# Moving operands of a one-core transformer block placed 32 to 224 bytes further on in a 256-byte line

## The chip, the cores and the metric

The kernel runs on one core of one Trainium2 chip. The metric is the device time in microseconds of one execution, as the median of several. TensorE (PE in the profile) multiplies a weight tile that it has loaded with a moving operand that it reads from SBUF column by column; the result goes to PSUM. VectorE (DVE) and ScalarE (ACT) do the element-wise work, and the queue of SyncE (SP) issues the loads from HBM.

## The reference

One layer over 512 tokens of width 1024: an input projection, a state-space mixer and a dilated attention side by side, both gated and projected back, a gated feed-forward part of width 2816 with a causal convolution of three taps, and a last gated addition.

```python
u = rms_norm(h, mix_norm_g)
z = u @ w_in                       # 1024 -> 512 + 3 * 768 + 2 * 1024
y_a = s5_mixer(z[:, :512], ...) @ w_branch_a     # inside: y * sigmoid(y @ glu_w + glu_b)
y_b = dilated_attention(q, k, v) @ w_branch_b
h = h + (g_a * y_a + g_b * y_b) @ w_out
u2 = rms_norm(h, ffn_norm_g)
gate = causal_depthwise_conv(u2 @ ffn_w_gate, ffn_conv_w, ffn_conv_b)
h = h + (gelu(gate) * (u2 @ ffn_w_up)) @ ffn_w_down
u3 = rms_norm(h, ple_norm_g)
h = h + sigmoid(u3 @ ple_w_gate) * (p @ ple_w_proj)
return rms_norm(h, final_norm_g)
```

## The kernel before

Activations lie in SBUF with 128 features on the partitions and all 512 tokens along the row, as float32. Every large product is made three times: each operand is split into a high part in TensorE's fp32r format and the rest as a low part, and `mm3` (lines 148 to 151) adds high times high (L149), high times low (L150) and low times high (L151). So each of the 128x128 weight tiles serves two matmuls with its high part and one with its low part, and each matmul has a weight load of its own.

The weights come in 132 chunks of 128x1024 floats through `wprep` (lines 115 to 131): a load into `wr`, ACT makes `wh` from it (L128), DVE makes `wl` (L129), three buffers of each in a ring. `gemm` takes eight weight tiles of 512 bytes a row out of a chunk, one after the other. The stages, in order, with the names that the rows show as result<-moving,weights:

- `pa`: five projections by tokens. Here the roles are the other way round: the weight chunk `wh`/`wl` moves, 512 columns of it, and slices of the activation `u1h`/`u1l` are loaded as weights.
- `v` and `gps`: the rest of the input projection, `u1h`/`u1l` moving. The small matmuls of the state-space mixer and of attention are woven in between by a list of background work that the program order fixes.
- `lps`: the mixer's gate, `yh`/`yl` moving; `bpb`: attention's projection, `bx` moving; `bpa`: the mixer's projection, `zh`/`zl` moving; `ops`: the output projection, `mh`/`ml` moving.
- twice (`part`): `pg` and `pu`, eleven pairs of feed-forward products with `u2h`/`u2l` moving, and `dps`, with `ah`/`al` moving.
- `pps`, with `px_` moving, and `eps`, with `u3h`/`u3l` moving; the last two rows of tiles of `eps` run in two halves of 256 columns each.
- `n_ps`, twice: a sum over partitions, `n_hi` and then `n_lo` moving, with the constant `ones_r` as weights (L241, L242).

The large activations lie in tagged slots of one pool (`slot`, line 76), used again by later stages. In the built program each slot, each `wr`, `wh`, `wl` and each 2 KB temporary, `n_hi` and `n_lo` among them, begins 64 bytes past a multiple of 256 in its partition's row; all steps from one tile to the next within them are multiples of 512 bytes. So weights and moving operand of each `mm3` begin at the same place in a line of 256 bytes. The constants `ones_r` and `cst` begin 160 and 224 bytes past a multiple of 256. `cst` is the weights of `shp` (L645), three small float32 products of the mixer's preparation, whose moving operand `pz` begins at 64.

Of the kernel before, what the change touches and what calls it, by code (L numbers as in the profile page):

```python
# [10 lines left out]
F32R = mybir.dt.float32r  # L11
# [9 lines left out]
SEQ = 512  # L21
# [22 lines left out]
STATS_AT = (7, 0)  # L44
NLAST = 2
LAST = ((0, 1), (2, 3))
LN2_HI = 0.693359375
LN2_LO = -2.12194440e-4

# [15 lines left out]
def tile_hybrid_block(ctx: ExitStack, tc: tile.TileContext, xT, xtok, pT, W, vecs, consts, ssm, out):  # L65
# [10 lines left out]
    def slot(i, shape, name, dt=F32):  # L76
        return sb.tile([P] + shape, dt, tag=f"s{i}", name=name)

    def small(shape, name, dt=F32):
        return sm_.tile([P] + shape, dt, tag=name, name=name)  # L80

    def mm_tile(name):
        return pm.tile([P, 512], F32, tag="mm", name=name)
# [4 lines left out]
    def t_tile(name):  # L88
        return ring.tile([P, 512], F32, tag="t", name=name, bufs=4)


    vec = small([V_N], "vec")
    nc.scalar.dma_start(vec, vecs)
    ones = small([128], "ones")
    DVE.memset(ones, 1.0)
    warm = small([1], "warm")
    ACT.activation(warm, ones[:, 0:1], AF.Sqrt)
    x = slot("x", [KD, SEQ], "x")
# [3 lines left out]
    def v1(col):  # L102
        return vec[:, col:col + 1]
# [47 lines left out]
        PE.matmul(ps, st[1], mv[0], start=False, stop=last)  # L151

    def u_tiles(name):
        uh = [slot(f"uh{j}", [4, SEQ], f"{name}h{j}", F32R) for j in range(2)]
        ul = [slot(f"ul{j}", [4, SEQ], f"{name}l{j}", F32R) for j in range(2)]
        return ([uh[k // 4][:, k % 4, :] for k in range(KD)], [ul[k // 4][:, k % 4, :] for k in range(KD)])

    def u_split(u, k, src, gcol, c=slice(0, SEQ)):
        ACT.activation(u[0][k][:, c], src[:, c], AF.Copy, scale=v1(gcol + k))  # L159
        DVE.scalar_tensor_tensor(u[1][k][:, c], src[:, c], v1(gcol + k), u[0][k][:, c].bitcast(F32), op0=ALU.mult, op1=ALU.subtract)  # L160
# [11 lines left out]
    def first():  # L172
        for c in (slice(0, 128), slice(128, SEQ)):
            nc.sync.dma_start(x[:, 0, c], xT[:, 0, c])
            u_split(u, 0, x[:, 0, :], V_MIX, c)

    u = u_tiles("u1")
    ready.append(wprep(2, first))
    load_x(1)
# [19 lines left out]
    def sq_acc(acc, k, src):  # L199
        if k == 0:  # L200
            ACT.activation(acc, src, AF.Square)
        else:
            t = t_tile("sq")
            ACT.activation(t, src, AF.Square)
            DVE.tensor_tensor(acc, acc, t, op=ALU.add)
# [29 lines left out]
    def rstd_full(acc, name):  # L235
        hi = ring.tile([P, SEQ], F32R, tag="t", name=name + "_hi", bufs=4)
        lo = ring.tile([P, SEQ], F32R, tag="t", name=name + "_lo", bufs=4)
        ACT.activation(hi, acc, AF.Copy)
        DVE.tensor_tensor(lo, acc, hi.bitcast(F32), op=ALU.subtract)
        ps = ax_tile(name + "_ps")  # L240
        PE.matmul(ps, ones_r, hi, start=True, stop=False)  # L241
        PE.matmul(ps, ones_r, lo, start=False, stop=True)  # L242
        m = t_tile(name + "_m")
        DVE.tensor_scalar(m, ps, 1.0 / D, EPS, op0=ALU.mult, op1=ALU.add)
        t = t_tile(name + "_t")
        ACT.activation(t, m, AF.Sqrt)
        y = sb.tile([P, SEQ], F32, tag="acc", name=name + "_y")
        DVE.reciprocal(y, t)
        DVE.tensor_tensor(t, y, y, op=ALU.mult)
        DVE.tensor_tensor(t, t, m, op=ALU.mult)  # L250
        DVE.tensor_scalar(t, t, -0.5, 1.5, op0=ALU.mult, op1=ALU.add)
        DVE.tensor_tensor(y, y, t, op=ALU.mult)
        return y
# [43 lines left out]
    S = slot("S", [NQ, 2, R, H], "S")  # L297
# [107 lines left out]
    def gemm(ps, kt, mv):  # L405
        for k in range(kt):
            mm3(ps, wT.next(), (mv[0][k], mv[1][k]), k == 0, k == kt - 1)
# [4 lines left out]
    def tt(o, a, b, op):  # L412
        DVE.tensor_tensor(o, a, b, op=op)  # L413
# [7 lines left out]
    def stt(o, a, s, b, o0, o1):  # L421
        DVE.scalar_tensor_tensor(o, a, s, b, op0=o0, op1=o1)

    def g_ssm():
# [12 lines left out]
        def rint(o, a, s):  # L437
            ts(o, a, s, ALU.mult, MAGIC, ALU.add)
            ts(o, o, -MAGIC, ALU.add)

        def exp_(o, a):
            xx, n, n1, r, q = e1, e2, e3, e4, e5
            ts(xx, a, -170.0, ALU.max, 170.0, ALU.min)
            rint(n, xx, LOG2E)
            stt(r, n, -LN2_HI, xx, ALU.mult, ALU.add)
            stt(r, n, -LN2_LO, r, ALU.mult, ALU.add)
# [439 lines left out]
    def split(hi, lo, src):  # L886
        ACT.activation(hi, src, AF.Copy)
        tt(lo, src, hi.bitcast(F32), ALU.subtract)

    yh = slot("S", [4, SEQ], "yh", F32R)  # L890
    yl = slot("f0", [4, SEQ], "yl", F32R)
    for k in range(4):
        split(yh[:, k, :], yl[:, k, :], yT[:, k, :])
    zh = slot("uh0", [4, SEQ], "zh", F32R)
    zl = slot("ul0", [4, SEQ], "zl", F32R)

    def parts(t, n):
        return [t[:, k, :] for k in range(n)]
# [1 line left out]
    for m in range(4):  # L900
        ps = mm_tile("lps")
        gemm(ps, 4, (parts(yh, 4), parts(yl, 4)))
        t = t_tile("lg")
# [8 lines left out]
    h = slot("x", [KD, SEQ], "h")  # L912
# [21 lines left out]


    u2 = u_tiles("u2")
    acc2 = sb.tile([P, SEQ], F32, tag="acc", name="acc2")
    for m in range(KD):
# [9 lines left out]
        DVE.memset(e[:, 0:2, 0:1], 0.0)  # L948
    u3 = None
    for part in range(2):  # L950
        ah = [slot(n, [4, SEQ], f"ah{part}{j}", F32R) for j, n in enumerate(("g0", "g1", "f0"))]
        al = [slot(n, [4, SEQ], f"al{part}{j}", F32R) for j, n in enumerate(("T", "f1", "S"))]
        a_h = [ah[k // 4][:, k % 4, :] for k in range(HALF)]
        a_l = [al[k // 4][:, k % 4, :] for k in range(HALF)]
        for mi in range(HALF):
            m = part * HALF + mi
            pg = mm_tile("pg")
            gemm(pg, KD, u2)
            if m == 0:
                rb2 = rstd_full(acc2, "n2")  # L960
            pu = mm_tile("pu")
            gemm(pu, KD, u2)
            e = exts[m % 2]
            tt(e[:, 2:6, :], pg.rearrange("p (r i) -> p r i", r=R), rb2.rearrange("p (r i) -> p r i", r=R), ALU.mult)
            ACT.activation(e[:, 0:2, 1:128], e[:, 4:6, 0:127], AF.Copy)
            t = t_tile("cv")
            t3 = t.rearrange("p (r i) -> p r i", r=R)
            ACT.activation(t3, e[:, 2:6, :], AF.Identity, bias=v1(V_CB + m), scale=v1(V_CW + 44 + m))
            stt(t3, e[:, 1:5, :], v1(V_CW + 22 + m), t3, ALU.mult, ALU.add)
            stt(t3, e[:, 0:4, :], v1(V_CW + m), t3, ALU.mult, ALU.add)  # L970
            ACT.activation(t, t, AF.Gelu_apprx_tanh)
            t2_ = t_tile("up")
            tt(t2_, pu, rb2, ALU.mult)
            tt(t, t, t2_, ALU.mult)
            split(a_h[mi], a_l[mi], t)
        if part == 1:
            u3 = u_tiles("u3")
            acc3 = sb.tile([P, SEQ], F32, tag="acc", name="acc3")
        for m in range(KD):
            ps = mm_tile("dps")  # L980
            gemm(ps, HALF, (a_h, a_l))
            tt(h[:, m, :], ps, h[:, m, :], ALU.add)
            if part == 1:
                u_split(u3, m, h[:, m, :], V_PLE)
                sq_acc(acc3, m, h[:, m, :])
# [67 lines left out]
    waiting = []  # L1053
    for gi, rs in enumerate(LAST):
        c = slice(rs[0] * 128, rs[-1] * 128 + 128)
        end = gi == len(LAST) - 1
        for m in tail:
# [19 lines left out]
    n = 0  # L1077
    for rs, y in zip(LAST, y4):
        for j in range(2):
# [153 lines left out]
```

## Time and profile before

| | |
|---|---|
| median of 3 runs | 808.01 us (807.91 to 808.68) |
| the profiled execution's own time | 807.97 us |
| its span, first to last instruction | 806.2 us |
| PE busy | 795.8 us, 4294 matmuls |
| PEld, weight loads | 659.8 us, 4294 loads |
| DVE busy | 489.8 us |
| ACT busy | 346.3 us |
| HBM read | 76.18 MB |

The profile is one execution. A matmul's record runs from its first column to a modelled end, after the next matmul has begun; so the records overlap, and the time from one start to the next is shorter than a record. A weight load (PEld) runs beside the matmul before its own.

### The profile page before, as it was taken

To read this page: it belongs to the slowest core of one execution; us is meant where nothing else is said; L and a number is where in the kernel's file an instruction comes from. 1 tells how busy PE (TensorE), PEld (TensorE's weight loads), DVE (VectorE), ACT (ScalarE), POOL (GpSimd) and SP (SyncE) were. 2 spreads that over 40 slices of the span, in tenths; PEclk is the share of its full clock that TensorE was granted. 3 is DMA by queue.
4 is the path that set the end of the run, shared out by engine and by line. 5 is a ranking of instruction groups with operands and counts; after the bars stand their busy time and mean duration, and the time that the engine had idled before them with its cause. 6 is when DMAs were issued, how large, how long until landed. Compare 5 with 4: busy or idle time off the path is not lost.

```text
span 806.2 us, 10860 instructions
## 1 busy us (share of the span) xinstructions
PE 795.8 (99%) x4294; PEld 659.8 (82%) x4294; DVE 489.8 (61%) x944; ACT 346.3 (43%) x551; POOL 10.9 (1%) x10
## 2 busy tenths in 40 slices
PE   9999999999999999999999999999999999999996
PEld 7888888788787788888888888888888888888886
DVE  6974799932544548756866556323655655445576
ACT  6763634434443533434544433221443443335464
POOL 2001000000000000000000000000000000000000
PEclk9999999999999999999999999999999999999999
DMA  7721121231111132533232232233223223222202
GB/s 272 273 91 62 46 93 63 80 105 53 53 54 54 53 105 81 206 105 114 96 105 91 93 104 96 88 104 105 80 103 105 95 89 104 99 87 102 102 4 104
DMA packets 23810, 78.97 MB, mean 98 GB/s; under 512 B 2640, under 2 KB 3024, under 8 KB 23760
## 3 DMA queue, kind: packets, MB, share of 16 engines
q1 hardware_dynamic: 23616, 78.22, 28.4%
q8 instruction: 33, 0.54, 0.3%
q14 instruction: 17, 0.14, 0.1%
q10 hardware_dynamic: 144, 0.07, 0.0%
HBM read 76.18 MB, written 2.10 MB: 97 GB/s over the span
## 4 chain that ended last, share of the span: by engine, by line
PE 86%; DVE 9%; ACT 2%; issue 1%; DMA 1%; SPq 0%; DVEq 0%; ACTq 0%
PE pu L151 5%; PE dps L151 5%; PE pg L151 5%; PE dps L150 5%; PE pu L149 5%; PE pu L150 5%; PE pg L149 5%; PE pg L150 5%; PE dps L149 5%; PE gps L149 4%; PE gps L151 4%; PE gps L150 4%; PE pa L151 2%; PE pa L150 2%; DVE E L413 2%; PE pa L149 2%
## 5 line engine op out<-in xcount | busy, mean ns | idle before, releaser
L128 ACT ACTIVATE wh<-wr 128x1024 fp32r<-128x1024 f32 (+1 forms) x132 | 138.1, 1047 | 302.0 <-issue 64.4
L129 DVE TENSOR_TENSOR wl<-wr,wh 128x1024 fp32r<-128x1024 f32 (+1 forms) x132 | 159.2, 1206 | 69.4 <-ACT wh L128 69.1
L150 PE MATMUL pu<-u2l,wh 128*128 128x512 f32 x176 | 68.5, 389 | 0.0
L149 PE MATMUL pu<-u2h,wh 128*128 128x512 f32 x176 | 68.5, 389 | 0.0
L149 PE MATMUL pg<-u2h,wh 128*128 128x512 f32 x176 | 68.5, 389 | 0.0
L150 PE MATMUL pg<-u2l,wh 128*128 128x512 f32 x176 | 68.5, 389 | 0.0
L151 PE MATMUL dps<-ah,wl 128*128 128x512 f32 x176 | 68.5, 389 | 0.0
L150 PE MATMUL dps<-al,wh 128*128 128x512 f32 x176 | 68.5, 389 | 0.0
L151 PE MATMUL pg<-u2h,wl 128*128 128x512 f32 x176 | 68.5, 389 | 0.0
L151 PE MATMUL pu<-u2h,wl 128*128 128x512 f32 x176 | 68.5, 389 | 0.0
L149 PE MATMUL dps<-ah,wh 128*128 128x512 f32 x176 | 68.5, 389 | 0.0
L149 PE MATMUL pa<-wh,u1h 128*128 128x512 f32 x160 | 63.2, 397 | 0.8 <-ACT u1h L159 0.7
L150 PE MATMUL pa<-wl,u1h 128*128 128x512 f32 x160 | 62.7, 392 | 0.0
L151 PE MATMUL pa<-wh,u1l 128*128 128x512 f32 x160 | 62.4, 392 | 0.1
L149 PE MATMUL gps<-u1h,wh 128*128 128x512 f32 x128 | 51.3, 401 | 0.0
L151 PE MATMUL gps<-u1h,wl 128*128 128x512 f32 x128 | 50.5, 395 | 0.0
L150 PE MATMUL gps<-u1l,wh 128*128 128x512 f32 x128 | 50.2, 392 | 0.0
L413 DVE TENSOR_TENSOR ext<-pg,n_y 128x512 f32<-128x512 f32 x22 | 15.2, 692 | 44.1 <-PE pg L151 44.1
L413 DVE TENSOR_TENSOR gt<-gps,n_bc 128x512 f32<-128x512 f32 x16 | 11.1, 692 | 50.7 <-PE gps L151 50.7
L150 PEld LDWEIGHTS dps<-al,wh 128*128 128x128 f32 x176 | 33.0, 188 | 6.9
L150 PEld LDWEIGHTS pu<-u2l,wh 128*128 128x128 f32 x176 | 33.0, 188 | 6.9
L150 PEld LDWEIGHTS pg<-u2l,wh 128*128 128x128 f32 x176 | 33.0, 188 | 6.9
(305 smaller groups left out, 1535.8 us busy)
## 6 DMA issues: line engine op xcount, KB each, us to landing
wr<-in_W_dram SPq DMA_DIRECT2D x128, 512.0 KB, 3.2
xt<-in_xtok_dram SPq DMA_DIRECT2D x4, 512.0 KB, 7.9
h<-in_xT_dram SPq DMA_DIRECT2D x8, 256.0 KB, 4.7
out_dram<-fo SPq DMA_DIRECT2D x8, 256.0 KB, 2.3
x<-in_xT_dram SPq DMA_DIRECT2D x7, 256.0 KB, 5.7
wr<-in_W_dram SPq DMA_DIRECT2D x4, 256.0 KB, 5.7
cst<-in_consts_dram SPq DMA_DIRECT2D x1, 568.0 KB, 10.4
sp<-in_ssm_dram SPq DMA_DIRECT2D x1, 544.0 KB, 7.5
```

What stands on the lines that cost most here:

```text
L128: ACT.activation(hi[:, c], raw[:, c], AF.Copy)
L129: DVE.tensor_tensor(lo[:, c], raw[:, c], hi[:, c].bitcast(F32), op=ALU.subtract)
L149: PE.matmul(ps, st[0], mv[0], start=first, stop=False)
L150: PE.matmul(ps, st[0], mv[1], start=False, stop=False)
L151: PE.matmul(ps, st[1], mv[0], start=False, stop=last)
L413: DVE.tensor_tensor(o, a, b, op=op)
```

## The change

A helper `moved` makes the tile 256 bytes longer than its content and lets the content begin `off` floats into it. The tiles `u1`, `u2`, `u3` (all three through `u_tiles`), `y`, `z` and `a` are made with it, at 32, 56, 8 and 16 floats: 128, 224, 32 and 64 bytes. The weights, `mh`/`ml`, `bx`, `px_`, `n_hi` and `n_lo` stay as they were. In the built program the instructions of each engine are the same and in the same order as before. Ten slots become 256 bytes longer, so that everything behind them lies some multiple of 256 bytes further on, and its place in a line of 256 bytes is unchanged. In `pa` the weights lie 128 bytes further on and the moving chunk does not; in the other stages it is the moving operand.

```diff
+U_OFF, Y_OFF, Z_OFF, A_OFF = 32, 56, 8, 16
...
+    def moved(tag, kt, name, off):
+
+        t = slot(tag, [kt * SEQ + 64], name, F32R)
+        return t[:, off:off + kt * SEQ].rearrange("p (k n) -> p k n", k=kt)
...
     def u_tiles(name):
-        uh = [slot(f"uh{j}", [4, SEQ], f"{name}h{j}", F32R) for j in range(2)]
-        ul = [slot(f"ul{j}", [4, SEQ], f"{name}l{j}", F32R) for j in range(2)]
+        uh = [moved(f"uh{j}", 4, f"{name}h{j}", U_OFF) for j in range(2)]
+        ul = [moved(f"ul{j}", 4, f"{name}l{j}", U_OFF) for j in range(2)]
...
-    yh = slot("S", [4, SEQ], "yh", F32R)
-    yl = slot("f0", [4, SEQ], "yl", F32R)
+    yh = moved("S", 4, "yh", Y_OFF)
+    yl = moved("f0", 4, "yl", Y_OFF)
...
-    zh = slot("uh0", [4, SEQ], "zh", F32R)
-    zl = slot("ul0", [4, SEQ], "zl", F32R)
+    zh = moved("uh0", 4, "zh", Z_OFF)
+    zl = moved("ul0", 4, "zl", Z_OFF)
...
-        ah = [slot(n, [4, SEQ], f"ah{part}{j}", F32R) for j, n in enumerate(("g0", "g1", "f0"))]
-        al = [slot(n, [4, SEQ], f"al{part}{j}", F32R) for j, n in enumerate(("T", "f1", "S"))]
+        ah = [moved(n, 4, f"ah{part}{j}", A_OFF) for j, n in enumerate(("g0", "g1", "f0"))]
+        al = [moved(n, 4, f"al{part}{j}", A_OFF) for j, n in enumerate(("T", "f1", "S"))]
```

## Rows read from the trace of the kernel before

**Rows 1.** The page's head: span, and busy time by engine.

```profile
span 806.2 us, 10860 instructions
PE 795.8 (99%) x4294; PEld 659.8 (82%) x4294; DVE 489.8 (61%) x944; ACT 346.3 (43%) x551; POOL 10.9 (1%) x10
```

**Rows 2.** All waits of PE: who for whom, total us, times, longest.

```profile
PE qkT L392 <- DVE qk L386: 1.6, 4, 0.8
PE warm L165 <- DVE apw L526: 1.0, 1, 1.0
PE pa L149 <- ACT u1h L159: 0.7, 2, 0.4
```

**Rows 3.** Busy time by stretch: us, PE busy (matmuls), granted clock, DMA share, GB/s.

```profile
0.00:20.00 20.00, 18.13 (x74) 1.00 0.77 271
20.00:40.00 20.00, 20.00 (x90) 1.00 0.74 272
520.00:540.00 20.00, 20.00 (x90) 1.00 0.26 84
```

**Rows 4.** The tile dps, 500 to 596 us: records min/median/max, first to last start.

```profile
L149 PE MATMUL dps<-ah,wh x87: 389/389/390, 499.7 to 558.2; 128*128 128x512 f32 x87
...
L151 PEld LDWEIGHTS dps<-ah,wl x87: 187/188/188, 499.9 to 558.4; 128*128 128x128 f32 x87
```

**Rows 5.** The tile shp: float32 matmuls of 256 columns, the same columns.

```profile
L645 PE MATMUL shp<-pz,cst x6: 378/379/380, 69.5 to 70.6; 128*128 128x256 f32 x6
```

**Rows 6.** The tile eps from 782 to 795 us: fp32r in halves.

```profile
L149 PE MATMUL eps<-u3h,wh x33: 277/283/389, 781.9 to 794.6; 128*128 128x256 f32 x32, 128*128 128x512 f32 x1
```

**Rows 7.** The tile n_ps, both times.

```profile
L241 PE MATMUL n_ps<-n_hi,ones_r x2: 392/392/393, 384.3 to 754.9; 128*128 128x512 f32 x2
L242 PE MATMUL n_ps<-n_lo,ones_r x2: 390/390/390, 384.5 to 755.1; 128*128 128x512 f32 x2
```

**Rows 8.** The tile pu, 384.7 to 386.7 us, just behind n_ps.

```profile
L149 PE MATMUL pu<-u2h,wh x3: 393/396/397, 384.7 to 386.1; 128*128 128x512 f32 x3
...
L150 PE MATMUL pu<-u2l,wh x3: 393/397/398, 385.0 to 386.4; 128*128 128x512 f32 x3
...
L151 PE MATMUL pu<-u2h,wl x3: 387/389/389, 385.2 to 386.6; 128*128 128x512 f32 x3
```

**Rows 9.** PE's groups of L149 by shape: count, busy us, mean ns, idle before.

```profile
L149 PE MATMUL pu<-u2h,wh 128*128 128x512 f32 x176 | 68.5, 389 | 0.0
L149 PE MATMUL pg<-u2h,wh 128*128 128x512 f32 x176 | 68.5, 389 | 0.0
L149 PE MATMUL dps<-ah,wh 128*128 128x512 f32 x176 | 68.5, 389 | 0.0
L149 PE MATMUL pa<-wh,u1h 128*128 128x512 f32 x160 | 63.2, 397 | 0.8 <-ACT u1h L159 0.7
L149 PE MATMUL gps<-u1h,wh 128*128 128x512 f32 x128 | 51.3, 401 | 0.0
L149 PE MATMUL ops<-mh,wh 128*128 128x512 f32 x64 | 24.9, 389 | 0.0
L149 PE MATMUL eps<-u3h,wh 128*128 128x512 f32 x48 | 18.7, 390 | 0.0
L149 PE MATMUL bpa<-zh,wh 128*128 128x512 f32 x32 | 12.5, 389 | 0.0
L149 PE MATMUL eps<-u3h,wh 128*128 128x256 f32 x32 | 9.1, 285 | 0.0
L149 PE MATMUL v<-u1h,wh 128*128 128x512 f32 x16 | 6.4, 400 | 0.0
L149 PE MATMUL bpb<-bx,wh 128*128 128x512 f32 x16 | 6.2, 390 | 0.0
L149 PE MATMUL pps<-px__5861,wh 128*128 128x512 f32 x16 | 6.2, 390 | 0.0
L149 PE MATMUL lps<-yh,wh 128*128 128x512 f32 x16 | 6.2, 389 | 0.0
```

## The prediction

> **What bounds the kernel now.** I read the page's head first: PE is busy in 795.8 of 806.2 us, DVE in 61% and ACT in 43% of the span [rows 1]. A busy PE need not be a PE at its peak, so the second view is its waits: 3.3 us in all, in seven places [rows 2]. No other engine and no transfer sets the pace after the first 20 us; a stretch in the middle has PE busy throughout, at a granted clock of 1.00 (the 2.4 GHz level) and with the DMA engines at 0.26 [rows 3]. So the time is the number of matmuls times the distance from one start to the next, and the question is what that distance consists of.
>
> For it I take one tile in a steady stretch. In `dps` the first and the last of 87 L149 matmuls start at 499.7 and 558.2 us, and between two of them stand one L150 and one L151: 58.5 us / (86 x 3) = 226.7 ns from start to start [rows 4]. The record of each is 389 ns, so a record outlasts the next start by about 162 ns, and differences between records can be read as differences between steps. The halves of `eps`, with 256 columns, have a median record of 283 [rows 6]: 256 columns more cost 106 ns, 0.414 ns each, one cycle at 2.4 GHz. 512 columns are then 213.3 ns, and about 13 ns of every step come once per matmul, whatever its columns. The weight load under it takes 188 ns [rows 4] and ends before the step does; it isn't the bound itself. But it comes once per matmul too, and it reads SBUF while the moving operand is read.
>
> Is the 13 ns a constant of the engine? Three rows say that it isn't quite. `shp`, float32 at half the pace of columns, has a record of 379, 10 ns less, and its moving operand, at 64, starts 96 bytes behind its weights, at 224, counted round a 256-byte line [rows 5]. `n_ps` takes its weights from `ones_r`, so that `n_hi`, at 64, starts 160 bytes behind them: its record is 392 both times, and the next is 390 [rows 7]. The `pu` matmuls right after it, back at distance 0, have records from 387 to 398 before they settle at 389 [rows 8], without any wait that the view of waits names there. So the step depends on how weight load and moving stream meet: 389 is where a long run at distance 0 settles, and records of this shape between 387 and 398 exist.
>
> **The change, part by part.** It adds and removes no instruction. ACT and DVE write the moved tiles at another start, with the same shapes; I cost that at nothing, under the 57% and 39% of the span in which these engines are idle [rows 1]. Without that cover a changed write would have to add more than the slack, and no row shows one that depends on its start. Ten slots 256 bytes longer cost nothing in time.
>
> What is left is the step of the matmuls whose distance changes. Each group of L149 has two like it, of L150 and L151, so three times the counts [rows 9]: with 512 columns `pu` 528, `pg` 528, `pa` 480, `gps` 384, `eps` 144, `v` 48, and `eps` in halves 96, together 2208 at distance 128; `dps` 528 at 64; `lps` 48 at 224 and `bpa` 96 at 32. That is 2880. Not moved are `ops` 192, `bpb` 48, `pps` 48.
>
> Price of one, from both sides. The best is the 379 of `shp`: 10 ns less [rows 5]. The worst is the 398 seen behind `n_ps`: 9 ns more [rows 8]. Nearer than either lie the shortest records of the same kind: 387 against 389 for 512 columns [rows 8], 277 against 283 for 256 [rows 6], 2 and 6 ns less. I take their mean, 4 ns less, for distance 128, which is as far from the weights as a 256-byte line allows; half of it, 2, for 64; a quarter, 1, for 32 and 224, which are 32 bytes away on either side. This proportion is my choice; no row fixes it.
>
> - distance 128: 2208 x 4 ns = 8.8 us
> - distance 64: 528 x 2 ns = 1.1 us
> - distances 32 and 224: 144 x 1 ns = 0.1 us
>
> Together 10.0 us less. Of the `pa` matmuls, those of the first 40 us run while the DMA engines are 0.74 to 0.77 busy [rows 3]; if the loads set the pace there, some 150 of them give nothing, 0.6 us, inside the rounding of the price. Elsewhere ACT and DVE have to bring the chunks 1.2% sooner, which their idle time allows. The profiled execution took 807.97 us, 1.8 us outside its span, and agrees with the median, 808.01; so 808.0 - 10.0 = **798.0 us**.
>
> **The rivals.**
>
> No change, 808. The weight load may have its own way into SBUF, and the 13 ns be the price of putting a new set of weights in place in this format. For it: all long runs settle at exactly 389, whatever slot, chunk buffer or stage [rows 9], though other address bits vary between them. The group means above 389, in `pa`, `gps` and `v`, come from stages with small matmuls woven in. Against it: rows 5, 7 and 8. The Trainium skill speaks for this rival: its page "TensorE: Matmul & The Clock Gate", in "Step-by-step: what each phase is for", gives PE two independent read ports and says that loading the next weights takes no SBUF bandwidth from the running matmul. By that rule the distance would be worth nothing and the time 808.0; the trace agrees only so far that the load is hidden, 188 ns in a step of 226.7.
>
> The whole excess goes, 779. Any distance other than 0 takes the two streams apart and the record falls to the 379 of `shp`: 2880 x 10 ns = 28.8 us, 779.2 us. For it: `shp` is the one full-width row at another distance with a long run of columns. Against it: it is float32, which reads its columns at half the pace, and `n_hi` at 160 is longer, not shorter.
>
> Slower, 817. The new distances settle above 389. The mechanism is the one of rows 7: the first fp32r matmul that this trace shows at a distance other than 0 has a record 3 ns longer, both times. At 3 ns each, 2880 x 3 = 8.6 us, 816.6 us; if the streams settled at the longest record, 9 ns, 833.9 us. It decides from the point at which the record of `pu` and `pg` lies above 389; these and the others at distance 128 are three quarters of all moved. Against it: two single matmuls at the start of a disturbance, which then swings to 387 as well, don't tell where a long run would settle.
>
> **How the numbers follow.** Partial gain 0.40, the whole excess 0.17, no change 0.19, slower 0.24. Anything within 0.2% (1.6 us) can't be told from no change. Faster is 0.40 + 0.17 = 0.57, same 0.19, slower 0.24. The partial gain's own range is 785 to 805. The range from 779 to 817 goes from the whole excess to 3 ns more per matmul; outside remain a gain past the record of `shp` and the part of the slower case beyond 392, together not over 0.2.
>
> **What the profile after would show.** The controls are in the kernel: `ops`, `bpb` and `pps` keep their distance and must stay at 389 or 390, and the record of `n_hi`, unmoved too, at about 392. Right would be: records of `pu`, `pg` and the 512-column `eps` near 385, `dps` near 387, `bpa` and `lps` near 388, with weight loads still near 188 and PE's waits still a few us. If they all stand at 389 and the time at 808, the excess isn't a meeting of the two streams, or doesn't hang on their distance in 256 bytes. If `pu` falls to 379, the price was too small by 6 ns. If it rises to 392 or more, the sign was wrong: distance 0 was already one of the better places. If the moved groups differ in another order than 128, 64, 32, the proportion is wrong. And if records fall but the span doesn't, a feeder has become the bound: DVE's `wl` (L129) or the loads of `wr` would then stand among PE's waits.

## The result and the profile after: slower by 1.5%

| | before | after |
|---|---|---|
| median, 4 runs each | 808.35 us (807.91 to 809.49) | 820.53 us (819.59 to 821.68) |
| span of the profiled execution | 806.2 us | 818.3 us |

The ratio is 1.0149, with a 95% interval of 1.0132 to 1.0167. The forecast was 798.0 us, in a range from 779 to 817.

The head of the page and all waits of PE after the change, to be read beside [rows 1, 2]:

```profile
span 818.3 us, 10860 instructions
PE 808.5 (99%) x4294; PEld 660.8 (81%) x4294; DVE 490.7 (60%) x944; ACT 346.7 (42%) x551; POOL 10.9 (1%) x10
```

```profile
PE warm L172 <- DVE apw L533: 1.0, 1, 1.0
PE qkT L399 <- DVE qk L393: 0.7, 2, 0.5
PE pa L156 <- ACT u1h L166: 0.6, 1, 0.6
PE pa L157 <- DVE u1l L167: 0.3, 1, 0.3
```

PE is 12.7 us busier, with the same 4294 matmuls and 2.6 us of waits instead of 3.3. ACT, DVE and the weight loads are as busy as before to within 1 us. So nothing new is waited for, and PE alone works clearly longer. The granted clock in a middle stretch is 1.00 as before (columns: stretch, its length, PE busy with its count, clock, DMA share, GB/s):

```profile
520.00:540.00 20.00, 20.00 (x90) 1.00 0.32 106
```

The groups of PE by shape, as [rows 9] (lines 149 to 151 are now 156 to 158):

```profile
L158 PE MATMUL pg<-u2h,wl 128*128 128x512 f32 x176 | 69.5, 395 | 0.0
L156 PE MATMUL pu<-u2h,wh 128*128 128x512 f32 x176 | 69.5, 395 | 0.0
...
L157 PE MATMUL dps<-al,wh 128*128 128x512 f32 x176 | 69.3, 394 | 0.0
L156 PE MATMUL dps<-ah,wh 128*128 128x512 f32 x176 | 69.0, 392 | 0.0
L158 PE MATMUL dps<-ah,wl 128*128 128x512 f32 x176 | 68.3, 388 | 0.0
L156 PE MATMUL pa<-wh,u1h 128*128 128x512 f32 x160 | 63.7, 400 | 0.7 <-ACT u1h L166 0.6
...
L156 PE MATMUL gps<-u1h,wh 128*128 128x512 f32 x128 | 51.7, 404 | 0.0
...
L156 PE MATMUL ops<-mh,wh 128*128 128x512 f32 x64 | 24.9, 389 | 0.0
...
L156 PE MATMUL eps<-u3h,wh 128*128 128x512 f32 x48 | 18.9, 395 | 0.0
L156 PE MATMUL bpa<-zh,wh 128*128 128x512 f32 x32 | 12.7, 396 | 0.0
L156 PE MATMUL eps<-u3h,wh 128*128 128x256 f32 x32 | 9.1, 284 | 0.0
...
L156 PE MATMUL bpb<-bx,wh 128*128 128x512 f32 x16 | 6.4, 398 | 0.0
L157 PE MATMUL pps<-px__5861,wh 128*128 128x512 f32 x16 | 6.3, 396 | 0.0
L156 PE MATMUL lps<-yh,wh 128*128 128x512 f32 x16 | 6.3, 396 | 0.0
```

Every moved group of 512 columns is longer, and `ops`, which was not moved, is at 389 as before. That the step (the time from one start to the next) grew, and not only the modelled record, is read from the first and last starts of one tile (columns: min/median/max, first to last start). The first row is `pg` in the second part after the change, the second the same of the kernel before; eleven groups of 24 matmuls with ten `pu` groups between make 501 steps from the first to the last L156:

```profile
L156 PE MATMUL pg<-u2h,wh x88: 390/393/404, 566.8 to 683.2; 128*128 128x512 f32 x88
```

```profile
L149 PE MATMUL pg<-u2h,wh x88: 389/389/390, 558.8 to 672.4; 128*128 128x512 f32 x88
```

116.4 us / 501 = 232.3 ns against 113.6 / 501 = 226.7. For `dps`, in the first part, and the two matmuls of `n_ps`:

```profile
L156 PE MATMUL dps<-ah,wh x88: 392/392/397, 506.3 to 566.1; 128*128 128x512 f32 x88
L157 PEld LDWEIGHTS dps<-al,wh x88: 188/188/188, 506.3 to 566.1; 128*128 128x128 f32 x88
...
L158 PE MATMUL dps<-ah,wl x88: 388/388/398, 506.8 to 566.5; 128*128 128x512 f32 x88
```

```profile
L248 PE MATMUL n_ps<-n_hi,ones_r x2: 389/389/389, 388.7 to 766.6; 128*128 128x512 f32 x2
...
L249 PE MATMUL n_ps<-n_lo,ones_r x2: 397/397/397, 389.0 to 766.8; 128*128 128x512 f32 x2
```

`dps`: 59.8 us / 261 steps = 229.1 ns, and its three lines differ steadily, 392, 394 and 388: the stage has settled into a repeating pattern, where before all three were 389 [rows 4]. The weight loads take 188 ns as before.

The sum by records: `pg` and `pu` 1056 x 5.7 ns = 6.0 us; `pa` 480 x 4.0 = 1.9; `gps` 384 x 3.7 = 1.4; `eps` in full width 144 x 5.0 = 0.7; `dps` 528 x 2.3 = 1.2; `lps` and `bpa` 144 x 6.3 = 0.9; `v` 48 x 4.3 = 0.2; `bpb`, unmoved, 48 x 3.7 = 0.2; and the halves of `eps` 96 x 1.7 = 0.2 less (means over the three lines of each). Together 12.3 us; the span grew by 12.1.

### The profile page after: what moved, and what is told of

Read it like the earlier page. It is cut to its first block, busy times and chain, and to the rows that moved or that the text cites. A ratio compares the mean times of both kernels' runs of the same rounds, so it can differ in the third digit from the quotient of the medians.

```text
span 818.3 us, 10860 instructions
## 1 busy us (share of the span) xinstructions
PE 808.5 (99%) x4294; PEld 660.8 (81%) x4294; DVE 490.7 (60%) x944; ACT 346.7 (42%) x551; POOL 10.9 (1%) x10
## 4 chain that ended last, share of the span: by engine, by line
PE 90%; DVE 6%; ACT 2%; issue 1%; DMA 1%; SPq 0%; DVEq 0%; ACTq 0%
PE pg L158 5%; PE pg L157 5%; PE pu L158 5%; PE pu L157 5%; PE pu L156 5%; PE pg L156 5%; PE dps L157 5%; PE dps L156 5%; PE dps L158 5%; PE gps L156 4%; PE gps L158 4%; PE gps L157 4%; PE pa L158 3%; PE pa L157 3%; PE pa L156 3%; PE ops L156 2%
## 5 line engine op out<-in xcount | busy, mean ns | idle before, releaser
L158 PE MATMUL pg<-u2h,wl 128*128 128x512 f32 x176 | 69.5, 395 | 0.0
L156 PE MATMUL pu<-u2h,wh 128*128 128x512 f32 x176 | 69.5, 395 | 0.0
L156 PE MATMUL pg<-u2h,wh 128*128 128x512 f32 x176 | 69.4, 394 | 0.0
L158 PE MATMUL pu<-u2h,wl 128*128 128x512 f32 x176 | 69.4, 394 | 0.0
L156 PE MATMUL dps<-ah,wh 128*128 128x512 f32 x176 | 69.0, 392 | 0.0
L158 PE MATMUL dps<-ah,wl 128*128 128x512 f32 x176 | 68.3, 388 | 0.0
L156 PE MATMUL pa<-wh,u1h 128*128 128x512 f32 x160 | 63.7, 400 | 0.7 <-ACT u1h L166 0.6
L158 PE MATMUL pa<-wh,u1l 128*128 128x512 f32 x160 | 63.1, 396 | 0.1
L156 PE MATMUL gps<-u1h,wh 128*128 128x512 f32 x128 | 51.7, 404 | 0.0
L158 PE MATMUL gps<-u1h,wl 128*128 128x512 f32 x128 | 51.0, 399 | 0.0
L420 DVE TENSOR_TENSOR up<-pu,n_y 128x512 f32<-128x512 f32 x22 | 15.2, 691 | 40.4 <-PE pu L158 40.4
```

Of the source, the lines that this page charges most:

```text
L156: PE.matmul(ps, st[0], mv[0], start=first, stop=False)
```

## The experiments

Theory: the step is set by the distance, in a line of 256 bytes, between the moving operand and the weights, and 0 is a good one. Rivals: it is the absolute place of the moving operand; or longer slots and other writes slow something else; or each distance is better or worse by its own conflicts between 128 columns of weights and the stream. Each kernel below takes a table of offsets by name in place of the change's four constants, in floats (4 bytes); a name that isn't in it has 0. All have the longer slots, except where said.

**base128: all distances 0, everything 128 bytes further on.** All offsets 0, and a spare tile ahead of the pools:

```diff
+    small([32], "space")
     ones = small([128], "ones")
```

Expected: 

> All distances are 0 again, but everything in the pools (weights, moving operands, temporaries) begins 192 instead of 64 bytes past a multiple of 256. If the distance between weights and moving operand sets the step, pg, pu, dps and ops stand at records of 389 and the time is that of the kernel before, 808 us. If the absolute place of the moving operand in its 256 bytes sets it (in the changed kernel u began at 192, and had records of 394 to 395), all stages are like pg after the change: about 3100 steps longer by 5.8 ns, 825 us or more.

Measured: 808.79 us against 808.80 of the kernel before, ratio 1.0000 (0.9990 to 1.0009). `pg`:

```profile
L157 PE MATMUL pg<-u2h,wh x176: 389/389/389, 378.7 to 672.2; 128*128 128x512 f32 x176
```

So neither the place 192, at which the u tiles lay in the changed kernel too, nor the longer slots cost anything. Of the rivals, the absolute place is out.

**no_u: the u tiles back.**

```diff
-U_OFF, Y_OFF, Z_OFF, A_OFF = 32, 56, 8, 16
+OFFS = {'u1h': 0, 'u1l': 0, 'u2h': 0, 'u2l': 0, 'u3h': 0, 'u3l': 0, 'ah0': 16, 'al0': 16, 'ah1': 16, 'al1': 16, 'yh': 56, 'yl': 56, 'zh': 8, 'zl': 8}
```

Expected: 

> Only y, z and a keep their offsets (224, 32 and 64 bytes); u1, u2, u3 are back at distance 0. By the records of the changed kernel, dps 528 steps by 2.3 ns, lps and bpa 144 by 6.6 ns: 2.2 us, so 810.2 us; the u tiles then carry the other 10 us. Rival, that a slower writer or the shift of the slots costs something in all stages: pg, pu and ops stay above 389 and the time above 812.

Measured: 811.05 us, ratio 1.0032 (1.0019 to 1.0045), 2.25 us above 808.80; 2.2 were expected. So the effects by stage add up within the interval of 1.5 to 3.6 us, and four fifths of the loss belong to the u tiles.

```profile
L156 PE MATMUL dps<-ah,wh 128*128 128x512 f32 x176 | 69.4, 394 | 0.0
L156 PE MATMUL pg<-u2h,wh 128*128 128x512 f32 x176 | 68.5, 389 | 0.0
...
L156 PE MATMUL bpa<-zh,wh 128*128 128x512 f32 x32 | 12.7, 396 | 0.0
L156 PE MATMUL lps<-yh,wh 128*128 128x512 f32 x16 | 6.3, 396 | 0.0
```

**weights192: the weights moved instead, and a moved along with them.** Slots are longer here only where the offset isn't 0.

```diff
-        hi = ring.tile([P, 1024], F32R, tag="wh", name=f"wh{i}", bufs=3)
-        lo = ring.tile([P, 1024], F32R, tag="wl", name=f"wl{i}", bufs=3)
+        hi = ring.tile([P, 1088], F32R, tag="wh", name=f"wh{i}", bufs=3)[:, 48:1072]
+        lo = ring.tile([P, 1088], F32R, tag="wl", name=f"wl{i}", bufs=3)[:, 48:1072]
...
+OFFS = {..., 'ah0': 48, 'al0': 48, 'ah1': 48, 'al1': 48, ...}
```

Expected: 

> Here the weight buffers wh and wl begin 192 bytes further on, u1, u2, u3, m, bx and px stay, and a is moved by 192 as well. If only the distance counts, moving behind weights: pg, pu, gps, ops, eps at 64 have steps of 229.0 ns like dps at 64 after the change; dps at 0 has 226.7, although both its operands lie elsewhere than ever before; pa at 192 (the weight chunk moves there) has 233. Rival, that moving operands must begin at 64 past 256: pg, pu and ops stay at 226.7 and dps rises.

Measured: 813.91 us in one run, beside 809.17 of the kernel before. `dps` and then `ops`:

```profile
L156 PE MATMUL dps<-ah,wh x88: 389/389/395, 503.1 to 562.3; 128*128 128x512 f32 x88
```

```profile
L156 PE MATMUL ops<-mh,wh x64: 388/388/388, 337.8 to 381.1; 128*128 128x512 f32 x64
L157 PE MATMUL ops<-ml,wh x64: 392/392/392, 338.1 to 381.3; 128*128 128x512 f32 x64
L158 PE MATMUL ops<-mh,wl x64: 394/394/394, 338.3 to 381.6; 128*128 128x512 f32 x64
```

`dps`, with both operands moved, is back at 59.2 / 261 = 226.8 ns. `ops`, none of whose moving operands was touched, has 43.3 / 189 = 229.1 ns and the pattern that `dps` had after the change at the same distance of 64, records of 388, 392 and 394 in turn, begun at another line. `pg` in the second part has 114.7 / 501 = 228.9. What counts is the difference of the two places, whichever of them is moved.

**scan1 and scan4: the other steps of 16 bytes.** In scan1 u1 16, u2 160, u3 240, a 96 and 192, y 16, z 240 bytes; in scan4 u2 112, u3 48, a 80 and 144, y 208, z 176.

```diff
+OFFS = {'u1h': 4, 'u1l': 4, 'u2h': 40, 'u2l': 40, 'u3h': 60, 'u3l': 60, 'ah0': 24, 'al0': 24, 'ah1': 48, 'al1': 48, 'yh': 4, 'yl': 4, 'zh': 60, 'zl': 60}
```

Expected of scan1: 

> Other distances, one for each stage: u1 (pa, gps) 16 bytes, u2 (pg, pu) 160, u3 (eps) 240, a 96 in the first part and 192 in the second, y 16, z 240. If any distance other than 0 spoils a meeting that only 0 has, all steps lie between 229 and 234 ns. If it is a matter of which distance, some lie below 226.7; then that one is the better kernel. If 16 bytes is too little to matter, pa and gps are at 226.7 to 228.

Expected of scan4: 

> The steps of 16 bytes not tried so far: u2 112, u3 48, a 80 and 144, y 208, z 176; u1 0. If 0 is the one good distance, all lie between 229 and 235 ns. A distance below 226.7 ns, if there is one, has to be among these or those of scan3; it would make a kernel faster than both.

**scan3: less than 16 bytes.** u2 8, u3 252, a 4 and 248, y 12, z 244; the line of code is alike.

Expected: 

> Distances of less than a 16-byte step, forward and back: u2 (pg, pu) 8 bytes, u3 (eps) 252, a 4 in the first part and 248 in the second, y 12, z 244; u1 0. If the two reads meet in pieces of 16 bytes, and only the piece of the start counts, 4, 8 and 12 are like 0 (226.7 ns a step) and 244 to 252 like 240 (226.7 or 233). If distance counts by the byte, they lie between, and one may be below 226.7.

Measured: 822.86 us (scan1), 817.47 (scan4) and 822.10 (scan3), one run each. `ops`, unmoved in all three, has its median record of 389 in each. All distances together, with those of the change, for matmuls of 512 columns; a step is worked out from first and last starts (tiles `pg`, `dps`, `lps`) or, where marked, as the mean record of the three lines less 162 ns. The starts are shown to 0.1 us, which leaves 0.2 ns open for `pg`, 0.4 for `dps`, and 2 for the short `lps` (12, 16 and 208 bytes):

| distance, bytes | step, ns | distance, bytes | step, ns |
|---|---|---|---|
| 0 | 226.7 | 128 | 232.3 |
| 4 | 238.0 | 144 | 233.3 |
| 8 | 233.3 | 160 | 234.3 |
| 12 | 229 | 176 | 231 (record) |
| 16 | 231 | 192 | 233.3 |
| 32 | 233 (record) | 208 | 236 |
| 48 | 234 (record) | 224 | 233 (record) |
| 64 | 229.1 | 240 | 226.5 or 233, and more (below) |
| 80 | 231.4 | 244 | 236 (record) |
| 96 | 233.3 | 248 | 233.0 |
| 112 | 230.9 | 252 | 230 (record) |

The row for 4 bytes, `dps` in the first part of scan3, 60.7 us / 255 steps:

```profile
L156 PE MATMUL dps<-ah,wh x86: 394/401/403, 504.2 to 564.9; 128*128 128x512 f32 x86
```

No distance is clearly below 0; only the better step of 240 equals it within the rounding. Four bytes are enough to lose 11 ns, so that pieces of 16 bytes, as scan3 had them for one outcome, don't explain it. There is no smooth course either: 4 is the worst, 12 among the mildest. None of the three kernels is faster than the one before.

In the halves of `eps`, with 256 columns, it is the other way round: 0 is the slowest of the distances tried. These are the first and the 87th matmul of the run of halves, in the kernel before (distance 0), after the change (128) and in scan3 (252); columns: start, length, both in us:

```profile
782.61 0.28 PE L149 MATMUL eps<-u3h,wh 128*128 128x256 f32 x1
...
792.92 0.28 PE L151 MATMUL eps<-u3h,wl 128*128 128x256 f32 x1
```

```profile
794.91 0.28 PE L156 MATMUL eps<-u3h,wh 128*128 128x256 f32 x1
...
805.12 0.28 PE L158 MATMUL eps<-u3h,wl 128*128 128x256 f32 x1
```

```profile
796.34 0.28 PE L156 MATMUL eps<-u3h,wh 128*128 128x256 f32 x1
...
806.37 0.28 PE L158 MATMUL eps<-u3h,wl 128*128 128x256 f32 x1
```

10.31 us / 86 steps = 119.9 ns at 0, 10.21 / 86 = 118.7 at 128, and 10.03 / 86 = 116.6 at 252. Read in the same way, 240 (scan1) has 117.1, 48 (scan4) 118.4 and 64 (weights192) 117.9, while base128, again at 0, has 119.9. So which distance is good depends on the number of columns that move.

**scan2: high and low parts at different distances** (u2 0 and 128, u3 128 and 0, a 0 and 64, then 64 and 0, y 0 and 32, z 0 and 192).

Expected: 

> High and low moving parts at different distances (bytes, high and low): u2 0 and 128, u3 128 and 0, a 0 and 64 in the first part, 64 and 0 in the second, y 0 and 32, z 0 and 192; u1 both 0. Of three matmuls, one moves the low part and two the high part. If each matmul pays for its own distance, pg and pu lose a third of the 5.8 ns (228.6), eps two thirds (230.5), the first dps a third of 2.3 (227.4), the second two thirds (228.2). If the steps settle jointly on a pattern of several matmuls, they don't add up like that, and some combination can be below 226.7.

Measured: 819.03 us in one run. `pg` has 116.9 / 501 = 233.3 ns, worse than with both parts at 128, although only one matmul in three has another distance; its lines:

```profile
L156 PE MATMUL pg<-u2h,wh x88: 387/397/398, 564.5 to 681.4; 128*128 128x512 f32 x88
L157 PE MATMUL pg<-u2l,wh x88: 392/395/395, 564.7 to 681.6; 128*128 128x512 f32 x88
L158 PE MATMUL pg<-u2h,wl x88: 388/392/393, 564.9 to 681.8; 128*128 128x512 f32 x88
```

L156 and L158 move the high part, at distance 0, and yet have medians of 397 and 392 in place of 389. The sum of a third of the price, 228.6, is refuted: the steps settle jointly.

**all240: one distance, several steps.** All moved operands at 240 bytes (60 floats).

Expected: 

> All moved operands at 240 bytes, 16 short of a full line. In the first scan eps at 240 had mostly steps of 226.7 ns, as at distance 0, and bpa at 240 had 233.3. If each distance has one step of its own, all stages agree here. If a distance has several patterns that repeat themselves and the stage's first matmuls decide which, some stages stand at 226.7 and others at 233, and a stage can change between them; the time then lies between 808 and 822 us.

Measured: 813.51 us in one run. `pg` in the first 5 us of its first group, and in the second part; then `pu` right behind that first group, `bpa` and `lps`:

```profile
L156 PE MATMUL pg<-u2h,wh x8: 396/396/396, 383.0 to 387.9; 128*128 128x512 f32 x8
```

```profile
L156 PE MATMUL pg<-u2h,wh x88: 388/388/389, 563.2 to 676.7; 128*128 128x512 f32 x88
```

```profile
L156 PE MATMUL pu<-u2h,wh x8: 388/388/389, 389.1 to 393.8; 128*128 128x512 f32 x8
```

```profile
L156 PE MATMUL bpa<-zh,wh x32: 396/396/397, 308.9 to 338.8; 128*128 128x512 f32 x32
```

```profile
L156 PE MATMUL lps<-yh,wh x16: 398/400/403, 294.8 to 305.5; 128*128 128x512 f32 x16
```

The first group of `pg` runs at 396, eight times over, 4.9 us / 21 = 233 ns. Later groups, with the same operand tiles, the same distance and the same instructions, run at 388 and 113.5 / 501 = 226.5 ns, which is the step of distance 0 within the rounding. Between the two lie the two matmuls of `n_ps`, at 388.6 and 388.8 us; `pu`, the next, is at 388 from its start. `bpa` stays at 396 throughout, and `lps`, at the same distance, at 400. So a distance has more than one pattern that repeats itself. That the matmuls before decide which is the likeliest reading, since operands and instructions of `pg` stay the same; it wasn't tried apart.

**half_weights and quarter: fewer weight columns.** The weight tiles of `dps` have 64 and 32 of their 128 columns; the other output rows of this product are left out.

```diff
-            gemm(ps, HALF, (a_h, a_l))
-            tt(h[:, m, :], ps, h[:, m, :], ALU.add)
+            for k in range(HALF):
+                w = wT.next()
+                mm3(ps[0:64], (w[0][:, 0:64], w[1][:, 0:64]), (a_h[k], a_l[k]), k == 0, k == HALF - 1)
+            tt(h[0:64, m, :], ps[0:64], h[0:64, m, :], ALU.add)
```

In half_weights `a` has distance 0, then 96; in quarter the columns are 0 to 31 in the first part and 32 to 63 in the second, which puts the weights 128 bytes further on.

Expected of half_weights: 

> The weight tiles of dps have 64 of their 128 columns (half of the output rows of the down projection are left out), at distance 0 in the first part and 96 in the second. If the excess over 213.3 ns comes from reading the weights beside the moving operand, it falls with the columns: at distance 0 from 13.3 to 7 ns or less (a step of about 220), and the gap between distance 96 (233.3) and 0 (226.7) shrinks by half or more. If it is a fixed price of changing weights, both steps stay.

Expected of quarter: 

> The weight tiles of dps have 32 of their 128 columns (three quarters of the output rows of the down projection are left out): columns 0 to 31 in the first part, so distance 0, and 32 to 63 in the second, where the weights begin 128 bytes further on, so distance 128. Half of the columns had steps of 230.0 ns at distance 0, not fewer than all of them. If the excess comes with each weight line that is read beside the stream, a quarter must at last show it: below 220 ns at both distances, and alike. If it comes with the start of a stream, whatever the amount that follows, the steps stay between 224 and 235 and differ between the parts.

Measured: half_weights 811.24 us and quarter 811.54, one run each. First parts of both, half_weights first:

```profile
L156 PEld LDWEIGHTS dps<-ah,wh x88: 133/134/135, 499.8 to 559.8; 128*64 128x64 f32 x88
L156 PE MATMUL dps<-ah,wh x88: 389/393/398, 500.0 to 560.1; 128*64 128x512 f32 x88
```

```profile
L156 PE MATMUL dps<-ah,wh x88: 391/394/397, 499.0 to 559.4; 128*32 128x512 f32 x88
L157 PEld LDWEIGHTS dps<-al,wh x88: 107/108/112, 499.0 to 559.4; 128*32 128x32 f32 x88
```

The load shrinks from 188 to 134 and 108 ns, but the step at distance 0 grows: 60.1 / 261 = 230.3 ns with 64 columns, 60.4 / 261 = 231.4 with 32, against 226.7 with all. In the second parts it is 231.4 (64 columns, distance 96) and 231.0 (32 columns, 128), 1.9 and 1.3 less than with all columns at these distances. My picture of a price for each piece of weights that is read beside the stream falls: none of the four steps is below 220, at distance 0 less to read even brought more excess, and there the good place is gone in both. The excess isn't a fixed price either, since the steps moved; and the two parts of quarter, which the start of a stream should have told apart, differ by no more than the rounding of 0.4 ns.

## Why the prediction was wrong

**What bounds the kernel: right.** PE's steps set the time, with 3.3 us of waits before and 2.6 after. The step of 226.7 ns held, and so did the reading that its part of 13 ns isn't a constant. That this part is the same whatever the columns holds at distance 0 alone: at 128 it is 19.0 ns with 512 columns (232.3 less 213.3) and 12.0 with 256 (118.7 less 106.7). The 2880 moved matmuls were the right ones to count.

**No cost elsewhere: right.** base128 has the longer slots and no time lost.

**That the distance acts: right, and now shown.** For `ops`, weights192 moved only the other operand and found the same step and pattern at the same distance. The rival of no change is refuted. The Trainium skill, "TensorE: Matmul & The Clock Gate", "Step-by-step: what each phase is for", has independent read ports and no bandwidth lost to the next load. The trace doesn't agree with that independence for this kernel: 192 bytes on the weights' side alone changed `ops` from 389 to 388, 392 and 394, though it doesn't show what the two reads share.

**The step that failed: the price.** I wrote that I take the mean of the shortest records, "4 ns less, for distance 128", with half for 64 and a quarter for 32 and 224. Measured by records: 5.7 ns more for 128 (`pg`, `pu`), 2.3 more for 64, 6.3 more for 32 and 224. Sign, size and proportion were wrong for 512 columns. Only for the 96 halves was the sign right, 1.2 ns a step instead of the 4 that I had taken. Two faults lie in the price. The 387 and 277 were single values in a swing right after a disturbance [rows 6, 8], 277 being the very first half; I took them for places where a run could rest. In rows 8 the swing's other values, 393 to 398, were more numerous, and all nine together have a mean of 393, above 389 in the very rows that I used. And I took distance 0 for the worst place; the scans show that for 512 columns none of the other 21 distances tried is clearly better than its 226.7 ns.

**The rivals.** The slower case came, by the mechanism that I gave it and with its mark, `pg` and `pu` above 389. Its price was mis-sized: 3 ns from `n_hi` [rows 7], one or two matmuls into a disturbance, where 5.7 was the settled loss at distance 128. The 392 of `n_hi` was no price of its distance at all, since it went to 389 with its distance unchanged; that its sign came true is partly luck. That put its end at 816.6 us, 3.9 below the 820.5 measured, and the range with it. The whole-excess rival leaned on `shp` [rows 5]; that row stayed at 379, but no fp32r distance came near it.

**The controls.** `ops` stayed at 389. `n_hi` went to 389 and `n_lo` to 397, though neither they nor `ones_r` were moved in their line, and `bpb`, between two stages at 32, has 398 in one line where I had called for 390. So the record of a matmul depends on those beside it too, as all240 and scan2 suggest as well.

**Open.** What the two reads share, why a settled pattern at distance 0 costs 13 ns, and why the halves of 256 columns prefer other distances isn't shown. The columns of the weights don't scale it. Whether it is a matmul's own weights or those loaded under it whose place counts wasn't tried apart. A step clearly below 226.7 ns wasn't found for 512 columns.

## What to carry to other kernels

When PE is always busy, read its step from first and last starts and compare it with the columns; a remainder that comes once per matmul can hang on addresses. In a kernel of long fp32r runs of 512 columns, with a load of 128 weight columns under every matmul, begin all weights and moving operands at the same place in 256 bytes, and check after each new tile that this still holds; here a shift of 4 bytes took the step from 226.7 to 238.0 ns. With 256 columns the same place was the slowest, by up to 3.3 ns, and with 32 or 64 weight columns it lost its advantage: measure there again. A short record inside a disturbance is no price: take the mean of a settled run, or of the whole disturbance.

## What the runs showed that I had not expected

- One distance can have several settled steps: at 240 bytes `pg` ran at 396 and later at 388 with unchanged operands and instructions, and `lps` at 400.
- A shorter weight load, 108 instead of 188 ns, made the step at distance 0 longer, 231.4 instead of 226.7 ns.
- Halves of 256 columns gained where 512 columns lost: 118.7 ns a step in `eps` at distance 128 and 116.6 at 252, against 119.9 at 0.
